# Forget heads: running sums spread through HBM instead of by transposes, and the logits projected before the first values

## The chip, the core and the metric

The program runs on one core of a Trainium2 chip. The core has a matrix engine (TensorE, PE in the profile, with a row of its own for the loading of weights, PEld), two engines for elementwise work (VectorE or DVE, ScalarE or ACT), GpSimd (POOL), and SyncE (SP), which here only issues transfers. Sixteen DMA engines move data between HBM and the on-chip memory. A transfer is issued from the queue of an engine: SP's for nearly all of them, ACT's for the results, POOL's for two. The metric is the device time of one execution in microseconds; the median of three runs is compared.

## What is computed

One block of a decoder for 256 positions and a model width of 2048, in float32. The part that the change touches is the forgetting attention: six heads of 128 columns, each with a logit per position that says how much is forgotten.

```python
h = rms_norm(x, g_mix[l])
proj = h @ w_in[l]
fq, fk, fv, f_logit, sq, sk, sv, mq, gates = jnp.split(proj, cuts, axis=-1)
...
log_f = jax.nn.log_sigmoid(f_logit.astype(jnp.float32) + b_forget[l].astype(jnp.float32))
...
c = jnp.cumsum(log_f, axis=-1)
...
    s = jnp.einsum('bhqd,bhkd->bhqk', q_blk, k).astype(jnp.float32) * scale
    s = s + c_blk[..., :, None] - c[..., None, :]
    s = jnp.where(key_pos[None, :] <= q_pos[:, None], s, -jnp.inf)
    p = jax.nn.softmax(s, axis=-1)
    return jnp.einsum('bhqk,bhkd->bhqd', p.astype(v.dtype), v)
```

So a head needs its running sum c twice: at the query's position, which is one number for each partition (queries lie on the partitions), and at the key's position, which is a row of 256 numbers that every partition must hold. Besides these six heads there are six stick-breaking heads, four heads over a memory of 256 tokens, three gates, an output projection, and a feed-forward part with a short convolution.

## The kernel before

**Products.** A float32 weight is used as the sum of two parts, `hi` and `lo`. `piece` (L136) loads 128 x 1024 numbers into `raw` through SP (L141), ACT rounds them to `hi` (L142), and DVE subtracts to get `lo` (L143). Each product of a tile is three matmuls (`three`, L328 to L330): high by high, low activation by high weight, high activation by `lo`. There are four buffers each of `raw`, `hi` and `lo`, so a load waits until DVE is through with the piece four places earlier. `product` runs the 2048 input columns in eight pieces of two tiles, which makes 24 such groups of matmuls for a result of 256 x 512.

**The order of the projections.** `proj` is called for the memory queries (`mq`), then for the forget heads' columns: f0, f1 and f2 are their queries and keys, f3 (512 columns) the values of heads 0 to 3, and f4 (262 columns) the values of heads 4 and 5 and the six logits. Then come s0, s1 and s2 (queries and keys of the stick-breaking heads), s3 and s4 (their values), and the gates g. In the profile the digits of such names are left out (`f`, `raw_f`, `s`).

**Work beside the products.** After each piece `product` calls `tick`. It moves on a background generator that loads pairs of tiles of later weights into `staged` (L301, SP), adds them up (L249 to L251, DVE) and stores the sums to HBM (L292, SP), and up to two (later three) of the waiting generators: transposes of finished queries and keys (`heads_T`), attention heads, and `running_sums`. A scheduler then lays out each engine's instructions from this order and the dependences; every engine and every DMA queue runs its own list strictly in order, and semaphores join the lists.

**A forget head before.** `running_sums` (L844) multiplies the log-sigmoids by triangles of ones on PE (L847 to L849), and DVE copies the result to `cq` (L850, L851), which holds the sums by query. `fox_head` then makes the row by key: DVE copies the head's column to 128 x 256 (L863), PE transposes its two halves against the identity into the bank `fa` (L868, two instructions), and ACT copies the result from there to `ck` (L871). PE's two score products (L869, L870) stand behind the transposes. DVE adds and subtracts the sums (L874), POOL masks the diagonal (L875), and the softmax, three transposes and the product with the values follow (`softmax_rows`, L882 to L885, `weighted`). The generators of the sums and of the heads are queued after f4, so they run beside s0 to s3.

**Another place that spreads a row.** The feed-forward part needs one scale per position in every partition. It writes 256 numbers of 4 bytes to HBM through POOL's queue (`rstd_row`, L1103) and loads them into all partitions from there (`rbc`, L1104). It is the one such pair in the program before.

Of the kernel before, what the change touches and what calls it, by code (L numbers as in the profile page):

```python
# [9 lines left out]
F32 = mybir.dt.float32  # L10
F32R = mybir.dt.float32r
AF = mybir.ActivationFunctionType
ALU = mybir.AluOpType
AX = mybir.AxisListType

P = 128
S = 256
NT = S // P
# [3 lines left out]
N_FOX, N_SB, N_MEM = 6, 6, 4  # L22
# [20 lines left out]
def hybrid_block(  # L43
# [25 lines left out]
    nc = tc.nc  # L69
# [12 lines left out]
    def bank(name):  # L82
        return pp.tile([P, 512], F32, tag="bank", name=name)
# [14 lines left out]
    def later(gen):  # L98
        waiting.append(gen)
# [18 lines left out]
    issued = set()  # L118

    def until(*names):  # L120
        while not issued.issuperset(names):
            yield
# [34 lines left out]
    def product(x_of, w, nk, n0, n, name):  # L157

        ps = [bank(f"{name}_{t}") for t in range(NT)]
        wv = w.rearrange("(k p) n -> p k n", p=P)  # L160
        for k in range(0, nk, 2):
            a = min(2, nk - k)
            wh, wl = piece(wv[:, k : k + a, n0 : n0 + n], a, n, f"{name}_{k}")
            order = [(j, t) for j in range(a) for t in range(NT)]
            if k + a == nk:
                order.sort(key=lambda jt: jt[1])
            for j, t in order:
                xk = x_of(k + j)
                xs_ = xk[:, t * P : (t + 1) * P], xk[:, S + t * P : S + (t + 1) * P]
                three(ps[t][:, :n], *xs_, (wh[:, j], wl[:, j]), k + j == 0, k + j == nk - 1)  # L170
            tick()
        return ps

    def split_to(dst, src):

        nc.scalar.copy(dst[..., :S], src)
        nc.vector.tensor_tensor(dst[..., S:], src, dst[..., :S].bitcast(F32), ALU.subtract)
# [57 lines left out]
    dram = ctx.enter_context(tc.tile_pool(name="dram", bufs=1, space=bass.MemoryType.DRAM))  # L235
# [250 lines left out]
    ident = cst.tile([P, P], F32, name="ident")  # L486
# [112 lines left out]
    rstd, rneg, rstd_m, rstd_f = (scales[:, i] for i in range(4))  # L599
# [7 lines left out]
    gp = mix.enter_context(tc.tile_pool(name="gp", bufs=3))  # L607

    def block(name, dt=F32):
        return bp.tile([P, 1024], dt, tag="blk", name=name)  # L610
# [4 lines left out]
    def rows_of(b):  # L615
        return b.rearrange("p (t n) -> p t n", t=NT)
# [26 lines left out]
    def heads_T(y, dst, gs, delay, name):  # L643

        yield delay
        for pr in range(2):
            ps = bank(f"hT_{name}_{pr}")
            for j in range(2):
                for t in range(NT):
                    h = 2 * pr + j  # L650
                    nc.tensor.transpose(
                        ps[:, j * S + t * P : j * S + (t + 1) * P], y[:, t, h * HD : (h + 1) * HD], ident
                    )
            out_v = dst[:, 2 * pr : 2 * pr + 2].rearrange("p h s -> p (h s)")
            if gs[pr] is None:
                nc.vector.tensor_copy(out_v, ps)
            else:
                nc.vector.tensor_scalar(out_v, ps, gs[pr], None, ALU.mult)
            if pr == 0:
                yield  # L660
        issued.add(name)
# [54 lines left out]
    for k in range(KT):  # L716
# [18 lines left out]
        for _ in range(0 if k < 3 else 1 if k < 8 else 3):  # L735
            if squares:
                j, t = squares.popleft()
# [16 lines left out]
    proj = lambda n0, n, name: product(xT, w_in[0], KT, n0, n, name)  # L754
    oT = op.tile([P, N_FOX + N_SB + N_MEM, 2 * S], F32R, tag="ot", name="oT")

    def softmax_rows(dst, src, name):
        nm = sm.tile([P, 1], F32, tag="nm", name=f"nm_{name}")
        nc.vector.tensor_reduce(nm, src, AX.X, ALU.max, negate=True)
        rs = sm.tile([P, 1], F32, tag="rs", name=f"rs_{name}")  # L760
        nc.scalar.activation(dst, src, AF.Exp, bias=nm, accum_out=rs)
        nc.vector.reciprocal(rs, rs)
        nc.vector.tensor_scalar(dst, dst, rs, None, ALU.mult)

    def weighted(pT, v, h, oh, o):

        c = slice((h % 4) * HD, (h % 4 + 1) * HD)
        vh = v[h // 4]
        nc.tensor.matmul(o[:, :S], lhsT=vh[:, 0, c], rhs=pT[:, :S], start=True, stop=False)
        nc.tensor.matmul(o[:, P:S], lhsT=vh[:, 1, c], rhs=pT[:, S : S + P], start=False, stop=True)  # L770
        split_to(oT[:, oh, :], o[:, :S])


    ps = proj(C_MQ, MEM_W, "mq")
# [40 lines left out]
    vf = [None] * 2  # L815
    for c in range(3):
        ps = proj(c * 512, 512, f"f{c}")
# [4 lines left out]
            for h in range(N_MEM):  # L822
                later(mem_head(h))
        later(heads_T(y, qk[c], gs, 2, f"f{c}"))
    ps = proj(1536, 512, "f3")
    vf[0] = rows_of(block("vf0"))
    for t in range(NT):
        nc.scalar.activation(vf[0][:, t], ps[t], AF.Copy, scale=rstd[:, t : t + 1])
    ps = proj(2048, 262, "f4")
    vf[1] = rows_of(block("vf1"))  # L830
    logits = cst.tile([P, 4, NT * N_FOX], F32, name="logits").rearrange("p i (t h) -> p i t h", t=NT)
    fl, lf, ab, cq = (logits[:, i] for i in range(4))
# [8 lines left out]
    nc.scalar.activation(ab, ab, AF.Ln, bias=1.0)  # L841
    nc.vector.scalar_tensor_tensor(lf, fl, 0.0, ab, ALU.min, ALU.subtract)

    def running_sums():  # L844
        yield 2
        cps = bank("cps")
        nc.tensor.matmul(cps[:, :N_FOX], lhsT=upto, rhs=lf[:, 0], start=True, stop=True)  # L847
        nc.tensor.matmul(cps[:, 8 : 8 + N_FOX], lhsT=ones, rhs=lf[:, 0], start=True, stop=False)
        nc.tensor.matmul(cps[:, 8 : 8 + N_FOX], lhsT=upto, rhs=lf[:, 1], start=False, stop=True)  # L849
        nc.vector.tensor_copy(cq[:, 0], cps[:, :N_FOX])  # L850
        nc.vector.tensor_copy(cq[:, 1], cps[:, 8 : 8 + N_FOX])  # L851
        issued.add("sums")

    def fox_head(h):
        yield from until("sums", "f0", "f1", "f2")
        q, k = qk[h // 4][:, h % 4], qk[(N_FOX + h) // 4][:, (N_FOX + h) % 4]
        b = block(f"fx_{h}")
        cb = b[:, :S].rearrange("p (j s) -> p j s", j=NT)
        ck = b[:, S : 2 * S]
        s = (b[:, 2 * S : 2 * S + P], b[:, 2 * S + P : 3 * S + P])  # L860
        pT = b[:, : 3 * P]

        nc.vector.tensor_copy(cb, cq[:, :, h : h + 1].to_broadcast([P, NT, P]))  # L863
        yield
        A = bank(f"fa_{h}")
        B = bank(f"fb_{h}")
        for j in range(NT):
            nc.tensor.transpose(A[:, j * P : (j + 1) * P], cb[:, j], ident)  # L868
        nc.tensor.matmul(B[:, :P], lhsT=q[:, :P], rhs=k[:, :P], start=True, stop=True)  # L869
        nc.tensor.matmul(A[:, S:], lhsT=q[:, P:], rhs=k, start=True, stop=True)  # L870
        nc.scalar.copy(ck, A[:, :S])  # L871
        for i, sp in enumerate((B[:, :P], A[:, S:])):
            nk = (i + 1) * P
            nc.vector.scalar_tensor_tensor(s[i], sp, cq[:, i, h : h + 1], ck[:, :nk], ALU.add, ALU.subtract)  # L874
            nc.gpsimd.affine_select(  # L875
                s[i][:, nk - P :], s[i][:, nk - P :], pattern=[[-1, P]], compare_op=ALU.is_ge,
                fill=NEG, base=0, channel_multiplier=1,
            )
            softmax_rows(s[i], s[i], f"f{h}_{i}")
        yield 3  # L880
        tp = B[:, P:]
        nc.tensor.transpose(tp[:, :P], s[0], ident)  # L882
        nc.tensor.transpose(tp[:, P : 2 * P], s[1][:, :P], ident)
        nc.tensor.transpose(tp[:, 2 * P :], s[1][:, P:], ident)
        nc.vector.tensor_copy(pT, tp)  # L885
        yield
        weighted(pT, vf, h, h, A)

    later(running_sums())
    for h in range(N_FOX):  # L890
        later(fox_head(h))

# [2 lines left out]
    for c in range(3):  # L895
        ps = proj(C_SB + c * 512, 512, f"s{c}")
# [52 lines left out]
    ps = proj(C_SB + 1536, 512, "s3")  # L949
# [4 lines left out]
    ps = proj(C_SB + 2048, 256, "s4")  # L954
# [56 lines left out]
    for m in range(2):  # L1011
        gate = []
        for b, plan in enumerate(g_plans[m]):
# [41 lines left out]
            if not plan:  # L1055
                biases()
                for n in range(2):
                    ps = proj(c0 + n * 512, 512, f"g{n}_{b}")
# [12 lines left out]
        for n in range(2):  # L1071
            acc = gate[branches[0][3]][n]
            for i, (w, k0, nk, b) in enumerate(branches):
                ps = product(lambda k: oT[:, k0 + k], w[0], nk, (2 * m + n) * 512, 512, f"b{2 * m + n}_{b}")
# [141 lines left out]
    for f0 in range(0, FT, 4):  # L1216
# [5 lines left out]
        for s in range(2):  # L1222
            ps = [bank(f"u{f0 + i}_{s}") for i in range(4)]
# [118 lines left out]
```

## Time and profile before

| what | value |
|---|---|
| three runs, us | 1461.80, 1462.06, 1462.67 (median 1462.06) |
| the profiled execution, us | 1461.49 |
| span from its first to its last instruction, us | 1459.8 |
| granted TensorE clock over the span | 1.000 |
| PE busy, share of the span | 1454.0 us, 100% |
| DVE, ACT, POOL busy | 1213.4 us, 850.0 us, 19.3 us |
| moved by DMA | 381.08 MB, 261 GB/s on average |

All times inside the program are microseconds from the span's start. A row of the view of groups or of one tile names line, engine, operation, result and operands, shape and count, with the duration of one. A row of the timeline gives start, duration, engine, line, operation and, in brackets, how long the engine stood idle before it and for what. In the view by stages each row is a stretch of time with the busy time of each engine in it, the granted clock, the share of the DMA engines' time that packets took, and the rate at which they moved data.

### The profile page before, as it was taken

What the parts mean: (1) busy time and instruction counts of PE and PEld (TensorE: products, weight loads), DVE (VectorE), ACT (ScalarE), POOL (GpSimd) and SP (SyncE); (2) the same over time, 40 slices, a digit from 0 to 9 for tenths busy, and PEclk for the clock granted to TensorE, in tenths of its full rate; (3) what the DMA queues carried; (4) which work ended last, traced back from release to release, by engine and by line L of the source; (5) the groups of instructions that cost most, each with busy time, mean ns of one, the idle gap of its engine ahead of it and who ended that gap; (6) DMA issues with size and microseconds to landing.
All of it is one profiled execution on the core that took longest, in us unless ns stands there. A gap on an engine that the chain in (4) does not pass through costs nothing.

```text
span 1459.8 us, 20547 instructions
## 1 busy us (share of the span) xinstructions
PE 1454.0 (100%) x7314; PEld 1230.1 (84%) x7314; DVE 1213.4 (83%) x1791; ACT 850.0 (58%) x1212; POOL 19.3 (1%) x48
## 2 busy tenths in 40 slices
PE   9999999999999999999999999999999999999998
PEld 7888888888888888888888888888888888888887
DVE  5778777776898899997887888888888877999878
ACT  6755454564564555545666556556556565676665
POOL 0000000010000000000000000000000000000000
PEclk9999999999999999999999999999999999999999
DMA  9697798777668576788877888888888866899995
GB/s 312 202 330 248 267 341 288 238 241 222 209 207 269 172 231 198 270 265 263 276 196 232 288 266 306 278 273 299 283 281 298 267 200 202 253 291 333 299 324 222
DMA packets 162534, 381.08 MB, mean 261 GB/s; under 512 B 12234, under 2 KB 27486, under 8 KB 158334
## 3 DMA queue, kind: packets, MB, share of 16 engines
q1 hardware_dynamic: 161022, 377.52, 78.9%
q10 hardware_dynamic: 1328, 2.11, 0.4%
q8 instruction: 57, 0.93, 0.3%
q14 instruction: 47, 0.39, 0.1%
q0 software_dynamic: 80, 0.13, 0.0%
HBM read 343.01 MB, written 36.70 MB: 260 GB/s over the span
## 4 chain that ended last, share of the span: by engine, by line
PE 97%; DVE 1%; DMA 1%; issue 0%; SPq 0%; ACT 0%; DVEq 0%; ACTq 0%
PE u L1231 22%; PE u L1232 11%; PE xd L329 3%; PE xd L330 3%; PE xd L328 3%; PE xg L330 3%; PE xg L329 3%; PE xg L328 3%; PE s L328 2%; PE s L330 2%; PE f L330 2%; PE f L328 2%; PE f L329 2%; PE s L329 2%; PE b L330 2%; PE b L328 2%
## 5 line engine op out<-in xcount | busy, mean ns | idle before, releaser
L1231 PE MATMUL u<-hT,hi_u 128*128 128x512 f32 x1232 | 428.3, 394 | 0.0
L1232 PE MATMUL u<-hT,lo_u 128*128 128x256 f32 x1232 | 341.3, 277 | 0.0
L1231 PEld LDWEIGHTS u<-hT,hi_u 128*128 128x128 f32 x1232 | 231.0, 188 | 53.8
L143 DVE TENSOR_TENSOR lo_u<-raw_u,hi_u 128x1024 fp32r<-128x1024 f32 x176 | 215.1, 1222 | 73.2 <-ACT hi_u L142 71.9
L142 ACT CAST hi_u<-raw_u 128x1024 fp32r<-128x1024 f32 x176 | 184.7, 1050 | 135.0 <-PE u L1231 106.7
L1232 PEld LDWEIGHTS u<-hT,lo_u 128*128 128x128 f32 x1232 | 231.2, 188 | 0.0
L323 DVE TENSOR_TENSOR lo_d<-raw_d,hi_d 128x1024 fp32r<-128x1024 f32 x88 | 106.7, 1222 | 16.2 <-ACT hi_d L322 13.8
L322 ACT CAST hi_d<-raw_d 128x1024 fp32r<-128x1024 f32 x88 | 91.7, 1053 | 38.8 <-PE xd L329 17.8
L322 ACT CAST hi_g<-raw_g 128x1024 fp32r<-128x1024 f32 (+1 forms) x80 | 77.1, 972 | 48.9 <-PE xg L329 19.2
L323 DVE TENSOR_TENSOR lo_g<-raw_g,hi_g 128x1024 fp32r<-128x1024 f32 (+1 forms) x80 | 88.6, 1119 | 4.1 <-ACT hi_g L322 4.1
L142 ACT CAST hi_f<-raw_f 128x1024 fp32r<-128x1024 f32 (+1 forms) x40 | 38.5, 967 | 51.8 <-PE f L329 42.8
L330 PE MATMUL xg<-lo_g,xT 128*128 128x512 f32 x175 | 68.1, 389 | 0.0
L329 PE MATMUL xg<-hi_g,xT 128*128 128x512 f32 x175 | 68.1, 389 | 0.0
L328 PE MATMUL xg<-hi_g,xT 128*128 128x512 f32 x175 | 68.1, 389 | 0.0
L143 DVE TENSOR_TENSOR lo_f<-raw_f,hi_f 128x1024 fp32r<-128x1024 f32 (+1 forms) x40 | 44.6, 1118 | 22.3 <-ACT hi_f L142 21.7
L143 DVE TENSOR_TENSOR lo_s<-raw_s,hi_s 128x1024 fp32r<-128x1024 f32 (+1 forms) x40 | 44.7, 1117 | 20.9 <-ACT hi_s L142 20.9
L1231 PE MATMUL u<-hT_rest,hi_u 128*128 128x512 f32 x176 | 62.0, 394 | 0.0
L142 ACT CAST hi_b<-raw_b 128x1024 fp32r<-128x1024 f32 x32 | 33.6, 1051 | 45.2 <-DMA raw_b<-in_w_br_fox_dram 15.8
L142 ACT CAST hi_s<-raw_s 128x1024 fp32r<-128x1024 f32 (+1 forms) x40 | 38.4, 961 | 36.8 <-PE s L329 23.9
L1182 ACT ACTIVATE y<-u,taps 128x256 f32<-128x256 f32 x88 | 49.6, 596 | 16.3 <-DVE u L1177 16.2
L330 PE MATMUL xd<-lo_d,aT 128*128 128x512 f32 x148 | 57.6, 389 | 0.0
L328 PE MATMUL xd<-hi_d,aT 128*128 128x512 f32 x148 | 57.6, 389 | 0.0
(520 smaller groups left out, 3473.1 us busy)
## 6 DMA issues: line engine op xcount, KB each, us to landing
raw_u<-in_w_up_dram SPq DMA_DIRECT2D x176, 512.0 KB, 4.5
raw_g<-in_w_in_dram SPq DMA_DIRECT2D x96, 512.0 KB, 4.4
raw_d<-in_w_down_dram SPq DMA_DIRECT2D x63, 512.0 KB, 5.4
pre_d<-in_w_down_dram SPq DMA_DIRECT2D x17, 1024.0 KB, 6.2
kept_d<-pre_d SPq DMA_DIRECT2D x17, 1024.0 KB, 6.2
raw_f<-in_w_in_dram SPq DMA_DIRECT2D x32, 512.0 KB, 4.9
raw_s<-in_w_in_dram SPq DMA_DIRECT2D x32, 512.0 KB, 5.2
raw_t_d<-kept_d SPq DMA_DIRECT2D x25, 512.0 KB, 5.8
```

The lines of the kernel that those rows point to most:

```text
L142: pin(nc.scalar.copy(hi[:, :m], raw[:, :m]))
L143: pin(nc.vector.tensor_tensor(lo[:, :m], raw[:, :m], hi[:, :m].bitcast(F32), ALU.subtract))
L322: nc.scalar.copy(hi[:, :n], src)
L323: nc.vector.tensor_tensor(lo[:, :n], src, hi[:, :n].bitcast(F32), ALU.subtract)
L328: fix(nc.tensor.matmul(o, lhsT=ah, rhs=w[0], start=first, stop=False))
L329: fix(nc.tensor.matmul(o, lhsT=al, rhs=w[0], start=False, stop=False))
L330: fix(nc.tensor.matmul(o, lhsT=ah, rhs=w[1], start=False, stop=last))
L1182: nc.scalar.activation(y, u[:, 2:], AF.Identity, scale=tap(2), bias=tap(3))
L1231: nc.tensor.matmul(ps[i], lhsT=hi[:, j, c], rhs=hT(k + j), start=first, stop=False)
L1232: nc.tensor.matmul(ps[i][:, :S], lhsT=lo[:, j, c], rhs=hT(k + j)[:, :S], start=False, stop=last)
```

## The change

Three things are done.

1. The projection f4 and the logits that come from it are placed ahead of f3. `running_sums` is queued right behind f4, and so runs beside f3; the six heads are queued after f3.
2. At the end of `running_sums` the sums go to HBM and back, in two parts: heads 0 to 3 (`ck_row4`, 4 KB) and heads 4 and 5 (`ck_row2`, 2 KB). The first two transfers write 256 runs of 16 bytes and 256 runs of 8 bytes. The other two load the whole row into each of the 128 partitions: `ck4`, 512 KB, into the one buffer tagged `pre`, and `ck2`, 256 KB, into one of the three tagged `bg`. All four are issued from POOL's queue, and each load waits for its own write.
3. A head no longer makes its row: DVE's spreading copy, the two transposes, ACT's copy and one step of waiting are gone, and the subtraction reads the loaded row. Before the product with the values a head checks that f3 has been written out.

```diff
-    ps = proj(1536, 512, "f3")
-    vf[0] = rows_of(block("vf0"))
-    for t in range(NT):
-        nc.scalar.activation(vf[0][:, t], ps[t], AF.Copy, scale=rstd[:, t : t + 1])
     ps = proj(2048, 262, "f4")
...
+    ck = [None] * N_FOX
+
     def running_sums():
         yield 2
...
         nc.vector.tensor_copy(cq[:, 1], cps[:, 8 : 8 + N_FOX])
+        for h0, n, tag, bufs in ((0, 4, "pre", 1), (4, 2, "bg", 3)):
+            row = dram.tile([S, n], F32, tag=f"ck_row{n}", name=f"ck_row{n}")
+            nc.gpsimd.dma_start(row.rearrange("(t p) h -> p t h", t=NT), cq[:, :, h0 : h0 + n])
+            every = gp.tile([P, S * n], F32, tag=tag, bufs=bufs, name=f"ck{n}")
+            nc.gpsimd.dma_start(every, row.rearrange("s h -> (s h)").partition_broadcast(P))
+            for h in range(n):
+                ck[h0 + h] = every.rearrange("p (s h) -> p h s", h=n)[:, h]
+        yield 5
         issued.add("sums")
+
+    later(running_sums())
+    ps = proj(1536, 512, "f3")
+    vf[0] = rows_of(block("vf0"))
+    for t in range(NT):
+        nc.scalar.activation(vf[0][:, t], ps[t], AF.Copy, scale=rstd[:, t : t + 1])
+    issued.add("vf0")
 
     def fox_head(h):
         yield from until("sums", "f0", "f1", "f2")
         q, k = qk[h // 4][:, h % 4], qk[(N_FOX + h) // 4][:, (N_FOX + h) % 4]
         b = block(f"fx_{h}")
-        cb = b[:, :S].rearrange("p (j s) -> p j s", j=NT)
-        ck = b[:, S : 2 * S]
...
-        nc.vector.tensor_copy(cb, cq[:, :, h : h + 1].to_broadcast([P, NT, P]))
-        yield
         A = bank(f"fa_{h}")
         B = bank(f"fb_{h}")
-        for j in range(NT):
-            nc.tensor.transpose(A[:, j * P : (j + 1) * P], cb[:, j], ident)
         nc.tensor.matmul(B[:, :P], lhsT=q[:, :P], rhs=k[:, :P], start=True, stop=True)
         nc.tensor.matmul(A[:, S:], lhsT=q[:, P:], rhs=k, start=True, stop=True)
-        nc.scalar.copy(ck, A[:, :S])
...
-            nc.vector.scalar_tensor_tensor(s[i], sp, cq[:, i, h : h + 1], ck[:, :nk], ALU.add, ALU.subtract)
+            nc.vector.scalar_tensor_tensor(s[i], sp, cq[:, i, h : h + 1], ck[h][:, :nk], ALU.add, ALU.subtract)
...
         nc.vector.tensor_copy(pT, tp)
         yield
+        yield from until("vf0")
         weighted(pT, vf, h, h, A)
 
-    later(running_sums())
     for h in range(N_FOX):
         later(fox_head(h))
```

The lists of the engines move as follows. In these rows the digits of a name are whole (`lo_f4_8` is the lo part of f4's piece that starts at tile 8), and the last number is that of the buffer.

First DVE, in the list of before, from the last `lo` that is made early for the projection behind f2 to the next one:

```order
L143 TENSOR_TENSOR lo_f3_6_1616<-raw_f3_6_1614,hi_f3_6_1615 128x1024
L631 TENSOR_REDUCE hss_f2_1524<-sq_f2_0_1525 128x4
L631 TENSOR_REDUCE hss_f2_1524<-sq_f2_1_1528 128x4
L658 TENSOR_SCALAR qk_fox0_1051<-hT_f0_1_1565,gh_109 128x512
L573 TENSOR_SCALAR nwa_f2_1532<-hss_f2_1524 128x8
L658 TENSOR_SCALAR qk_fox1_1313<-hT_f1_1_1571,gh_109 128x512
L576 TENSOR_TENSOR nwt_f2_1533<-nwy_f2_1534 128x8
L249 TENSOR_TENSOR staged_861<-staged_861 128x1024
L577 SCALAR_TENSOR_TENSOR nwt_f2_1533<-nwt_f2_1533,nwa_f2_1532 128x8
L143 TENSOR_TENSOR lo_f3_8_1637<-raw_f3_8_1635,hi_f3_8_1636 128x1024
```

The same place of DVE's list after the change, where the projection behind f2 is f4:

```order
L658 TENSOR_SCALAR qk_fox0_1051<-hT_f0_0_1508,gh_109 128x512
L658 TENSOR_SCALAR qk_fox1_1313<-hT_f1_0_1514,gh_109 128x512
L249 TENSOR_TENSOR staged_861<-staged_861 128x1024
L631 TENSOR_REDUCE hss_f2_1524<-sq_f2_0_1525 128x4
L631 TENSOR_REDUCE hss_f2_1524<-sq_f2_1_1528 128x4
L658 TENSOR_SCALAR qk_fox0_1051<-hT_f0_1_1565,gh_109 128x512
L573 TENSOR_SCALAR nwa_f2_1532<-hss_f2_1524 128x8
L658 TENSOR_SCALAR qk_fox1_1313<-hT_f1_1_1571,gh_109 128x512
L576 TENSOR_TENSOR nwt_f2_1533<-nwy_f2_1534 128x8
L250 TENSOR_TENSOR staged_861<-staged_861 128x512
L577 SCALAR_TENSOR_TENSOR nwt_f2_1533<-nwt_f2_1533,nwa_f2_1532 128x8
L143 TENSOR_TENSOR lo_f4_8_1637<-raw_f4_8_1635,hi_f4_8_1636 128x524
```

The evictions of heads (L658), the norms of f2 and the background sums stand now between pieces of f4, whose matmuls are half as wide as those of f3.

Second PE, in the list of before, where head 0's scores stand behind the piece s0_8:

```order
L330 MATMUL s0_1_1891<-lo_s0_8_1977,xT_432 128x512
L868 MATMUL fa_0_1993<-ident_78,fx_0_1973 128x128 x2
L869 MATMUL fb_0_1994<-qk_fox1_1313,qk_fox0_1051 128x128
L870 MATMUL fa_0_1993<-qk_fox1_1313,qk_fox0_1051 128x256
L328 MATMUL s0_0_1890<-hi_s0_10_2023,xT_432 128x512
```

The same scores in PE's list after the change:

```order
L330 MATMUL s0_1_1905<-lo_s0_2_1926,xT_432 128x512
L876 MATMUL fb_0_1944<-qk_fox1_1313,qk_fox0_1051 128x128
L877 MATMUL fa_0_1943<-qk_fox1_1313,qk_fox0_1051 128x256
L328 MATMUL s0_0_1904<-hi_s0_4_1968,xT_432 128x512
L329 MATMUL s0_0_1904<-hi_s0_4_1968,xT_432 128x512
```

The two transposes are gone, and the scores stand three pieces earlier, behind s0_2.

Third DVE again after the change, where the sums are copied out of PSUM and where they are used (`ck4` is the loaded row of heads 0 to 3):

```order
L848 COPY logits_1723<-cps_1809 128x6
L849 COPY logits_1723<-cps_1809 128x6
L143 TENSOR_TENSOR lo_f3_8_1825<-raw_f3_8_1823,hi_f3_8_1824 128x1024
L143 TENSOR_TENSOR lo_f3_10_1845<-raw_f3_10_1843,hi_f3_10_1844 128x1024
L143 TENSOR_TENSOR lo_f3_12_1864<-raw_f3_12_1862,hi_f3_12_1863 128x1024
L143 TENSOR_TENSOR lo_f3_14_1882<-raw_f3_14_1880,hi_f3_14_1881 128x1024
```

```order
L143 TENSOR_TENSOR lo_s0_4_1969<-raw_s0_4_1967,hi_s0_4_1968 128x1024
L143 TENSOR_TENSOR lo_s0_6_2014<-raw_s0_6_2012,hi_s0_6_2013 128x1024
L880 SCALAR_TENSOR_TENSOR fx_0_1942<-fb_0_1944,logits_1723,ck4_1817 128x128
L880 SCALAR_TENSOR_TENSOR fx_0_1942<-fa_0_1943,logits_1723,ck4_1817 128x256
L759 TENSOR_REDUCE nm_f0_0_1951<-fx_0_1942 128x1
L759 TENSOR_REDUCE nm_f0_1_1961<-fx_0_1942 128x1
```

The copies have moved from the middle of s0 to the middle of f3, and the four transfers wait for them; the first use of a loaded row stands on DVE between lo_s0_6 and lo_s0_8. On POOL's list the four transfers stand ahead of the mask of head 0. On SP's list the loads of the gates' biases (`bg`, L1019 before, L1025 after), which stood among the loads of the memory's weights at the start, stand now among those of s1 and s2, and the second and third of them directly ahead of the load of s2_12.

## The prediction

> **What bounds the kernel now.** I read the busy times first, then the chain that ended last, then the stretch from f3 to the middle of s1 by stages.
>
> ```profile
> span 1459.8 us, 20547 instructions
> PE 1454.0 (100%) x7314; PEld 1230.1 (84%) x7314; DVE 1213.4 (83%) x1791; ACT 850.0 (58%) x1212; POOL 19.3 (1%) x48
> PE 97%; DVE 1%; DMA 1%; issue 0%; SPq 0%; ACT 0%; DVEq 0%; ACTq 0%
> ```
>
> PE is busy for all but 6 us, and 97% of the chain is its own list. So two things count: matmul time taken off PE, and any wait that makes PE stand. Work taken from DVE or ACT is worth nothing by itself. The stages, with their DMA share and rate in the last two columns:
>
> ```profile
> 156.00:168.00 12.00, 12.00 (x63) 10.09 (x61) 11.28 (x19) 6.83 (x10) 0.00 (x0) 1.00 0.63 221
> 168.00:180.50 12.50, 12.50 (x61) 10.33 (x60) 10.14 (x15) 3.64 (x5) 0.00 (x0) 1.00 0.78 261
> 180.50:192.30 11.80, 11.80 (x98) 11.76 (x97) 7.76 (x10) 6.18 (x9) 0.00 (x0) 1.00 0.92 316
> 192.30:203.80 11.50, 11.50 (x56) 9.59 (x54) 5.80 (x8) 5.50 (x10) 0.00 (x0) 1.00 0.98 366
> 203.80:216.00 12.20, 12.20 (x60) 10.14 (x60) 11.56 (x29) 7.18 (x15) 2.35 (x4) 1.00 1.01 373
> ```
>
> The first two are f3, the third f4, the rest s0 and the start of s1. Because f4 uses its pieces twice as fast, the loads fall behind, and for the 24 us behind it the DMA engines are full at 366 to 373 GB/s. How near PE comes to standing there:
>
> ```profile
> ACT hi_s L142 <- DMA raw_s<-in_w_in_dram: 7.5, 8, 2.7
> 189.81 1.22 DVE L143 TENSOR_TENSOR lo_s<-raw_s,hi_s 128x1024 fp32r<-128x1024 f32 x1
> 192.78 0.39 PE L330 MATMUL s<-lo_s,xT 128*128 128x512 f32 x1
> ```
>
> ACT waits eight times for these loads. The first `lo` of s0 ends at 191.03 and is used at 192.78, a lead of 1.75 us. That is the least cover that I find there, and PE does not stand.
>
> **The change part by part: the transposes.** One head in the timeline of PE, and the two copies that go with it:
>
> ```profile
> 206.46 0.39 PE L330 MATMUL s<-lo_s,xT 128*128 128x512 f32 x1
> 206.69 0.38 PE L868 MATMUL fa<-ident,fx 128*128 128x128 f32 x2
> 206.90 0.39 PE L869 MATMUL fb<-qk_fox,qk_fox 128*128 128x128 f32 x2
> L863 DVE COPY fx<-logits x6: 274/286/289, 205.3 to 243.8; 128x256 f32<-128x256 f32 x6
> L871 ACT COPY fx<-fa x6: 351/373/374, 207.8 to 257.6; 128x256 f32<-128x256 f32 x6
> ```
>
> From L868 to L869 is 0.21 us of PE's list; six heads give **-1.26 us**, all on the path. DVE loses 6 x 0.29 and ACT 6 x 0.37 us; both lie beside PE and count nothing. The heads also start three pieces earlier and take a step less each; PE runs the same instructions, so I count that at nothing too. The check for f3's values costs nothing, since they are written out before a head reaches it.
>
> **The exchange of f3 and f4.** PE's matmuls are the same; what changes is what DVE must do beside them.
>
> ```profile
> 156.88 0.47 PE L328 MATMUL f<-hi_f,xT 128*128 128x512 f32 x1
> 157.39 0.74 DVE L658 TENSOR_SCALAR qk_fox<-hT_f,gh 128x512 f32<-128x512 f32 x1
> 163.05 1.22 DVE L143 TENSOR_TENSOR lo_f<-raw_f,hi_f 128x1024 fp32r<-128x1024 f32 x1
> 164.87 1.28 DVE L638 TENSOR_TENSOR y_f<-y_f,hr_f 128x512 f32<-128x512 f32 x2
> L143 DVE TENSOR_TENSOR lo_f<-raw_f,hi_f x13: 694/705/1219, 158.0 to 187.3; 128x524 fp32r<-128x524 f32 x8, 128x1024 fp32r<-128x1024 f32 x5
> ```
>
> Behind f2, DVE has evictions, norms and background sums; the fifth `lo` of f3 starts at 163.05. After the change that place loses a long `lo` (about 1.1 us to the next start) and gains a background sum (about 0.6), so f4's fifth `lo` ends near 162.5 + 0.7 = 163.2. A piece of f4 takes 11.8 / 8 = 1.47 us on PE, and four of them, with the eight transposes between, bring PE to its fifth `lo` at about 163.3: just in time. The next `lo` has a sum and two products of the norm ahead of it and comes about 2.6 us later, against 1.5 us of matmuls and some transposes that PE puts between. I take **+0.5 us**, and 0 to 1.5 as bounds.
>
> **The row through HBM.** The trace has one such pair, `rstd_row` and `rbc`:
>
> ```profile
> 761.13 0.86 POOL L1103 DMA_DIRECT2D rstd_row<-scales  x1 [421.83 <-DVE scales L578]
> 769.55 0.57 POOL L1104 DMA_DIRECT2D rbc<-rstd_row  x1 [7.55 <-DMA rstd_row<-scales]
> rbc<-rstd_row POOLq DMA_DIRECT2D x1, 128.0 KB, 7.2
> rstd_row<-scales POOLq DMA_DIRECT2D x1, 1.0 KB, 8.1
> 753.00:763.00 10.00, 10.00 (x60) 8.73 (x59) 6.76 (x16) 9.18 (x16) 0.86 (x1) 1.00 0.74 235
> 763.00:772.00 9.00, 9.00 (x54) 7.86 (x53) 4.91 (x7) 3.34 (x6) 0.57 (x1) 1.00 0.69 61
> 772.00:780.00 8.00, 8.00 (x48) 7.00 (x47) 3.87 (x4) 3.11 (x3) 0.00 (x0) 1.00 0.85 297
> ```
>
> The write of 1 KB takes 8.1 us, and while it runs everything else slows: 61 GB/s where the stretches around it have 235 and 297. It isn't that there was nothing to move. The loads of the feed-forward weights that SP issued from 740 to 762 us, then those from 762 to 770 us, and what ACT saw of them:
>
> ```profile
> DMA to landing us min/median/max: 3.6/3.6/4.0
> DMA to landing us min/median/max: 11.2/11.4/11.6
> ACT hi_u L142 <- DMA raw_u<-in_w_up_dram: 6.7, 2, 5.7
> ```
>
> Each load lands 7.8 us later than the ones before. Or by the rate: 9 us x (1 - 61 / 366) = **7.5 us** of a full DMA lost to one write of 256 small runs. There PE didn't stand, because its `hi` and `lo` were several pieces of some 3 us ahead. In f3, behind f4, they are not.
>
> The new writes are two, of 256 runs each, issued 0.86 us apart. PE starts f3 near 156 + 0.9 + 11.8 = 169 us; the copies of the sums stand on DVE behind the fourth `lo` of f3, near 178, so the writes run from about 180. That is 11 us behind f4's end, where the same distance in the program before is the row 203.80:216.00 with a full DMA. Lost DMA time is bounded by 0 (the larger runs pass at once) and 15 us (two writes in turn, each at the measured price). I take one price, 7.5, because the two overlap and because count and route are those of the measured one. The loads into all partitions add 0.79 MB, at 366 GB/s 2.1 us, less a cover of 1.75: PE stands for 7.5 + 2.1 - 1.75 = **+7.85 us** (bounds 0.35 and 15.35). Nothing gives this back, as the DMA is full before and after it.
>
> The Trainium skill, "DMA: Bandwidth & Descriptors", section "Anatomy of one DMA — SWDGE (gpsimd) path", fits a transfer from POOL's queue as 2.0 us plus its bytes at 436 GB/s. By that the write of 1 KB would take 2.0 us; the trace has 8.1, so here the trace decides. With the page's price and no slowing of others the sum would be that of the first rival. The same page's "Specifications" says that pieces under 512 B are read, modified and written; that speaks for a price by the number of runs, since 4, 8 and 16 bytes are alike below it.
>
> **What waits, and what is queued behind it.** POOL's four issues (2 x 0.86 + 2 x 0.57 us) and the wait for the writes stand ahead of head 0's mask:
>
> ```profile
> 208.59 0.69 POOL L875 TENSOR_SCALAR_AFFINE_SELECT fx<-fx 128x128 f32<-128x128 f32 x2 [206.44 <-DVE fx L874]
> ```
>
> POOL has been idle for 206 us there, which covers them. The row of heads 0 to 3 lands at about 178 + 8.1 + 0.6 + 7.2 + 1.8 = 196 us (the larger load takes 0.66 MB / 366 GB/s more). Its first use stands behind `lo_s0_6` and head 0's scores, PE's time 169 + 22 + 5.5 = 196.5 at the earliest. Should the row be late, DVE stands, and every `lo` from s0_8 on behind it; but the same slow DMA delays PE, so I add nothing. On SP's list two bias loads now stand ahead of s2_12's load and wait for head 5's subtraction; loads run several pieces ahead in that stretch, so nothing, at most 1 us.
>
> **The sum.** 1461.49 - 1.26 + 0.5 + 7.85 = 1468.6 for the profiled execution, whose span is 1459.8; it lies 0.57 under the median of the runs, so 1469.2, given as **1469**.
>
> **The rivals.** *The writes slow nothing, or are hidden* (the other side: not slower). The run of 16 or 8 bytes may pass quickly, or PE's lead may be larger than 1.75 us at that moment. Then -1.26 + 0.5 + 0.35 gives 1461.7. For it: one event is all that shows the slowing. Against: rate, landing and ACT's wait all agree on it. It decides below about 3 us of lost DMA. Chance 0.22.
> *Half the price* (runs four times as long, spread over 4 KB instead of 1): 3.75 lost, +3.3 in all, 1465.4. Chance 0.15.
> *One price*, my forecast: 1469. Chance 0.42.
> *Two in turn*: 15 us lost, 1476.7. For it: one queue carries both, and 512 runs are twice 256. Chance 0.18.
> *Faster by over 0.2%*, 2.9 us, about what a measurement of this kernel can tell from no change: the transposes give 1.26, and I know no other matmul time that goes. Chance 0.03.
>
> **Range and chances.** From the no-loss case to the doubled one, 1461 to 1477; about 0.15 lie outside. A third of the half-price case is within 0.2%, so: faster 0.03, same 0.26, slower 0.71. The likeliest case's own range is 1466 to 1472.
>
> **What would show it.** Right: a stretch of 6 to 15 us behind the writes with the rate well under 366 GB/s, ACT's waits for `raw_f` or `raw_s` longer by several us, and PE idle at `hi` or `lo` of late f3 or early s0; then heads of two products without L868. Wrong: the rate stays up there (the first rival), or PE stands at the products with the values or at head 0 because the row came late, or PE stands in f4 for several us behind DVE.

## The result, and the profile after

| what | before | after |
|---|---|---|
| median of 21 runs each, us | 1461.58 (1461.01 to 1465.18) | 1464.15 (1462.80 to 1466.80) |
| ratio, 95% interval | | 1.0018 [1.0012, 1.0024] |
| the profiled execution, us | 1461.49 | 1463.10 |
| its span, us | 1459.8 | 1461.4 |

The changed kernel is slower by 2.6 us, clear of the noise and on the side that I forecast, but by little more than a third of the 7 us that I forecast (1469 against the 1462.06 known then): 1464.15, inside the range of 1461 to 1477. The profiled execution is one of the faster ones of after (1.6 us over that of before), so what it shows lost is somewhat under the usual.

The page of after, its span, busy times and the chain of waits:

```profile
span 1461.4 us, 20527 instructions
PE 1454.0 (99%) x7302; PEld 1229.0 (84%) x7302; DVE 1211.1 (83%) x1785; ACT 848.7 (58%) x1206; POOL 20.8 (1%) x52
PE 95%; issue 2%; DVE 1%; DMA 1%; SPq 0%; POOL 0%; ACT 0%; POOLq 0%; DVEq 0%; ACTq 0%
```

PE has its twelve transposes fewer (7302 for 7314) and is still the bound. All its waits between 150 and 300 us (engine and line, what it waited for, us, times, longest); before, there were none:

```profile
PE f L328 <- ACT hi_f L142: 0.9, 1, 0.9
PE f L330 <- DVE lo_f L143: 0.5, 1, 0.5
PE s L330 <- DVE lo_s L143: 0.3, 1, 0.3
```

The first two stand at the last piece of f3, where PE's timeline reads:

```profile
190.52 0.39 PE L330 MATMUL f<-lo_f,xT 128*128 128x512 f32 x1
191.80 0.50 PE L328 MATMUL f<-hi_f,xT_rest 128*128 128x512 f32 x1 [0.89 <-ACT hi_f L142]
192.14 0.40 PE L329 MATMUL f<-hi_f,xT_rest 128*128 128x512 f32 x1
193.06 0.50 PE L330 MATMUL f<-lo_f,xT_rest 128*128 128x512 f32 x1 [0.52 <-DVE lo_f L143]
193.40 0.40 PE L328 MATMUL f<-hi_f,xT_rest 128*128 128x512 f32 x1
193.63 0.39 PE L329 MATMUL f<-hi_f,xT_rest 128*128 128x512 f32 x1
```

By the starts, 190.52 to 191.80 is 1.28 us where a step is 0.23, and 192.14 to 193.06 is 0.92: 1.05 + 0.69 us lost. That is more than the waits say, because a wait is counted from the end of the matmul before, which is 0.39 us behind that one's start, while the next matmul usually starts 0.23 us behind that start. The matmul behind a wait also takes 0.34 instead of 0.23 to its successor, another 0.11 each time. At 207.92 to 208.63, in s0, another 0.48 go. At the feed-forward part PE is 1.8 us later than before (745.0 and 743.2 us); with the transposes' 1.26 that is some 3 us lost in this profile.

What was going on then: POOL's transfers in its timeline, how long they took to land (the list of transfers; kind, count, size, us), and the stretches around them, DMA share and GB/s in the last two columns:

```profile
179.89 1.59 POOL L852 DMA_DIRECT2D ck_row<-logits  x2 [177.75 <-DVE logits L849]
187.09 0.57 POOL L854 DMA_DIRECT2D ck<-ck_row  x1 [5.61 <-DMA ck_row<-logits]
190.85 0.55 POOL L854 DMA_DIRECT2D ck<-ck_row  x1 [3.19 <-DMA ck_row<-logits]
```

```profile
ck<-ck_row POOLq DMA_DIRECT2D x1, 512.0 KB, 7.5
ck<-ck_row POOLq DMA_DIRECT2D x1, 256.0 KB, 6.6
ck_row<-logits POOLq DMA_DIRECT2D x1, 4.0 KB, 6.9
ck_row<-logits POOLq DMA_DIRECT2D x1, 2.0 KB, 9.8
```

```profile
168.00:180.00 12.00, 12.00 (x68) 10.28 (x67) 11.17 (x20) 6.74 (x10) 0.11 (x1) 1.00 0.98 376
182.00:194.00 12.00, 10.59 (x46) 8.15 (x45) 4.67 (x4) 4.36 (x5) 1.12 (x2) 1.00 0.99 279
```

The share of the DMA engines' time stays at 0.98 and 0.99 while the rate falls from 376 to 279 GB/s. Against 366 that is 12 x (1 - 279 / 366) = 2.9 us of DMA time; against the 328 to 347 of the kernels below that have no crowded writes in this stretch, mean 336, it is 2.0 us.

### The profile page after: what moved, and what is told of

The parts are those of the page before. It is cut to its first block, busy times and chain, and to the rows that moved or that the text cites. A ratio compares the mean times of both kernels' runs of the same rounds, so it can differ in the third digit from the quotient of the medians.

```text
span 1461.4 us, 20527 instructions
## 1 busy us (share of the span) xinstructions
PE 1454.0 (99%) x7302; PEld 1229.0 (84%) x7302; DVE 1211.1 (83%) x1785; ACT 848.7 (58%) x1206; POOL 20.8 (1%) x52
## 4 chain that ended last, share of the span: by engine, by line
PE 95%; issue 2%; DVE 1%; DMA 1%; SPq 0%; POOL 0%; ACT 0%; POOLq 0%; DVEq 0%; ACTq 0%
PE u L1237 22%; PE u L1238 11%; PE xg L330 4%; PE xg L328 4%; PE xg L329 4%; PE xd L330 3%; PE xd L328 3%; PE xd L329 3%; PE b L330 2%; PE b L328 2%; PE b L329 2%; PE s L328 2%; PE s L330 2%; PE s L329 2%; PE yd L330 2%
## 5 line engine op out<-in xcount | busy, mean ns | idle before, releaser
L142 ACT CAST hi_b<-raw_b 128x1024 fp32r<-128x1024 f32 x32 | 33.7, 1053 | 44.9 <-PE b L329 15.7
```

The costliest lines, as they stand in the source:

```text
L142: pin(nc.scalar.copy(hi[:, :m], raw[:, :m]))
```

## Experiments

Each median stands beside that of the kernel before, measured together with it. First, which part of the change costs. Theory W names the two writes, X the exchange of f3 and f4, L the loads into all partitions.

**The exchange alone.** The trip is taken out and the heads make their rows as before:

```diff
-        for h0, n, tag, bufs in ((0, 4, "pre", 1), (4, 2, "bg", 3)):
...
     def fox_head(h):
+        nc.vector.tensor_copy(cb, cq[:, :, h : h + 1].to_broadcast([P, NT, P]))
+        yield
...
+        for j in range(NT):
+            nc.tensor.transpose(A[:, j * P : (j + 1) * P], cb[:, j], ident)
...
+        nc.scalar.copy(ck, A[:, :S])
```

> The exchange of f3 and f4 alone: the sums run beside f3, but each head makes its row with DVE's copy, two transposes and ACT's copy as before, and no row goes through HBM. Theory W (the two writes of small runs take DMA time from the loads, and PE stands for it): no loss is left, 1461.6 to 1462.1 against 1461.6 before. Theory X (the exchange itself starves PE: loads and the lo parts come late behind f4): the loss stays and the transposes come back, 1464.2 + 1.26 = 1465.4. Theory L (the 0.79 MB of loads into all partitions are the cost): 1461.6 to 1462.1, as under W.

Measured: 1461.93 against 1461.89, ratio 0.9999 [0.9991, 1.0008]. Theory X falls. PE has no wait between 100 and 300 us. ACT waits for the loads of f3 there too, and it costs nothing:

```profile
ACT hi_f L142 <- DMA raw_f<-in_w_in_dram: 12.0, 7, 3.8
```

In after the same row has 15.7 us. So a long wait of ACT's for loads, by itself, doesn't tell that PE stands.

**The trip alone**, the two writes and two loads in the order of before:

```diff
         nc.vector.tensor_copy(cq[:, 1], cps[:, 8 : 8 + N_FOX])
+        for h0, n, tag, bufs in ((0, 4, "pre", 1), (4, 2, "bg", 3)):
...
+        yield 5
         issued.add("sums")
```

> The trip through HBM alone, in the order of before (f3, then f4; the sums beside s0, the four transfers from about 204 us on, heads a few pieces later). Theory W: the DMA engines are full there too (1.01 of their time at 204 to 216 us before), so the writes cost as in the changed kernel, some 3 us of DMA time less the lead, and the transposes give 1.26 back: 1462.5 to 1464. Theory X: nothing is exchanged, so the transposes' gain is left, 1460.3. Theory L: 2.1 us of load time less a lead of 1.75 and less 1.26: 1460.5 to 1461.

Measured: 1464.28 against 1461.89, ratio 1.0016 [1.0007, 1.0026], just above the 1464 that theory W allowed. The whole loss of the change comes with the trip, in another place of the program. PE stands once, at a `lo` of s0 some 20 us behind the writes:

```profile
231.99 0.50 PE L330 MATMUL s<-lo_s,xT 128*128 128x512 f32 x1 [1.98 <-DVE lo_s L143]
```

**The change without the writes:**

```diff
-            nc.gpsimd.dma_start(row.rearrange("(t p) h -> p t h", t=NT), cq[:, :, h0 : h0 + n])
-            nc.gpsimd.dma_start(every, row.rearrange("s h -> (s h)").partition_broadcast(P))
+            nc.gpsimd.tensor_copy(every[:, :1], cq[:, 0, :1])
+            nc.gpsimd.dma_start(every, b_gate[0, 0, : S * n].partition_broadcast(P))
```

> The changed kernel without the two writes; the loads into all partitions read rows of the gates' bias instead, behind a one-column copy on POOL that waits for the sums. The heads' forgetting term by key is therefore not computed from the logits. Theory W: the loss goes with the writes, and with only the loads left (2.1 us, lead 1.75) PE stands under 1 us: 1460.5 to 1461.5. Theory X: nothing changes, 1464.2. Theory L: nothing changes, 1464.2, and the loads start some 7 us earlier.

Measured: 1461.08 against 1461.89, ratio 0.9993 [0.9985, 1.0002]. The loads alone cost nothing that can be seen; theory L falls. The writes are what costs.

**The same trip with long runs.** One transpose of the sums on PE makes 12 rows of 128, and the writes carry 8 and 4 runs of 512 bytes:

```diff
+        nc.tensor.transpose(cps[: NT * N_FOX, P : 2 * P], cflat, ident)
+        cT = block("cT")[: NT * N_FOX, :P]
+        nc.vector.tensor_copy(cT, cps[: NT * N_FOX, P : 2 * P])
...
-            row = dram.tile([S, n], F32, tag=f"ck_row{n}", name=f"ck_row{n}")
-            nc.gpsimd.dma_start(row.rearrange("(t p) h -> p t h", t=NT), cq[:, :, h0 : h0 + n])
+            row = dram.tile([n * NT, P], F32, tag=f"ck_row{n}", name=f"ck_row{n}")
+            nc.gpsimd.dma_start(row, cT[h0 * NT : (h0 + n) * NT])
```

> The changed kernel with the same trip, but the sums are transposed once on PE first (12 columns, one instruction) and copied by DVE to 12 partitions, so that the two writes carry 8 and 4 runs of 512 bytes instead of 256 runs of 16 and 256 of 8. Theory W: the slowing goes with the number of small runs, so it goes away: 1460.7 to 1461.7. If instead any write from POOL's queue slows the others, whatever its runs, 1463.5 to 1464.5. Theories X and L: 1464.2 + 0.1.

> The kernel of the long runs once more, unchanged, to narrow its interval against the kernel before: 1460.8, 0.9992 of before, if the eleven transposes' 1.15 us are what it gains; 1461.5 to 1462 if the first comparison was luck.

Measured: 1460.81 against 1461.89, ratio 0.9992 [0.9983, 1.0001], and the second time 1461.71 against 1461.67, ratio 0.9999 [0.9990, 1.0009]. The loss is gone. Whether the eleven transposes' 1.15 us are gained isn't shown: the intervals hold both that and nothing. The stretch 182 to 194 us of this kernel, to be set beside that of after:

```profile
182.00:194.00 12.00, 12.00 (x55) 9.84 (x54) 8.56 (x10) 6.37 (x8) 2.31 (x4) 1.00 0.99 335
```

The same DMA share carries 335 GB/s, and PE is busy for all 12 us (in after, 10.59).

**The long runs in the order of before**, the same edit made to the trip alone:

```diff
-            nc.gpsimd.dma_start(row.rearrange("(t p) h -> p t h", t=NT), cq[:, :, h0 : h0 + n])
+            nc.gpsimd.dma_start(row, cT[h0 * NT : (h0 + n) * NT])
```

> The trip through HBM in the order of before (as in the trip alone), with the sums transposed once and written in 8 and 4 runs of 512 bytes. If crowded runs were all that the trip alone lost by, its 2.4 us go away and the twelve transposes less one are left: 1460.5 to 1461.2, as with the exchange. If the waits of DVE for late scores or rows cost there, 1462 to 1464.

Measured: 1461.13 against 1461.67, ratio 0.9999 [0.9990, 1.0008]. The trip alone loses nothing any more either.

**ACT's queue for the writes:**

```diff
-            nc.gpsimd.dma_start(row.rearrange("(t p) h -> p t h", t=NT), cq[:, :, h0 : h0 + n])
+            nc.scalar.dma_start(row.rearrange("(t p) h -> p t h", t=NT), cq[:, :, h0 : h0 + n])
```

> The changed kernel with the two writes issued from ACT's queue instead of POOL's; the loads stay on POOL's. If the slowing belongs to POOL's queue, it goes away: 1460.5 to 1461.5. If it belongs to the small runs, it stays: 1463.5 to 1465.

Measured: 1466.46 against 1462.18, ratio 1.0027 [1.0017, 1.0037]. The cost doesn't belong to POOL's queue. It is above the 1465 that I expected at most; whether it is larger than from POOL's isn't shown, since the interval overlaps that of after.

**Each write done twice**, the second time to a row that nobody reads:

```diff
             nc.gpsimd.dma_start(row.rearrange("(t p) h -> p t h", t=NT), cq[:, :, h0 : h0 + n])
+            again = dram.tile([S, n], F32, tag=f"again{n}", name=f"again{n}")
+            nc.gpsimd.dma_start(again.rearrange("(t p) h -> p t h", t=NT), cq[:, :, h0 : h0 + n])
```

> The changed kernel with each of the two writes done a second time to a row that nobody reads. If the lost DMA time adds up (2.9 us for the first pair by the rate) and PE pays for all of it, now that its lead is used up, 1464.2 + 2.9 = 1467.1, between 1466 and 1468. If the writes overlap and only the first pair matters, 1464.2 to 1465.

Measured: 1467.20 against 1462.18, ratio 1.0029 [1.0018, 1.0040]. The second pair costs about 0.0011 x 1462 = 1.6 us more by the ratios and 3.0 by the medians. That is what adding prices would give, or nearly, but it isn't shown: the intervals of the two ratios overlap.

Now why two writes cost less than my price for one. **My price at this place:** the kernel of the long runs with a write of 256 runs of 4 bytes into 1 KB, like `rstd_row`, ahead of its own:

```diff
+            if h0 == 0:
+                extra = dram.tile([NT, P], F32, tag="extra", name="extra")
+                nc.gpsimd.dma_start(extra.rearrange("t p -> p t"), cq[:, :, 0])
```

> The kernel of the long runs (1460.8, PE stands 0.1 us) with one more write ahead of its two: 256 runs of 4 bytes packed into 1 KB, as the write measured before, which nobody reads. If my price of 7.5 us of DMA time for such a write holds at this place, PE stands for 5.75 to 7.5 us: 1466.5 to 1468.3. If a write costs here what one of the changed kernel's did, about half of the 2.9 us that their two took, 1461 to 1462.3.

Measured: 1466.93 against 1462.18, ratio 1.0030 [1.0020, 1.0040]; over the kernel of the long runs 1466.93 - 1461.25 (the median of its 22 runs) = 5.7 us. So in time a write of this kind costs here about what I had priced. The stretch behind it, in an execution of 1469.91 us:

```profile
188.00:190.00 2.00, 2.00 (x11) 1.65 (x10) 0.91 (x1) 1.05 (x1) 0.00 (x0) 1.00 2.09 164
190.00:192.00 2.00, 2.00 (x11) 1.65 (x10) 0.32 (x1) 0.00 (x0) 0.00 (x0) 1.00 0.78 93
192.00:194.00 2.00, 1.06 (x5) 0.56 (x3) 0.00 (x0) 0.00 (x0) 0.00 (x0) 1.00 0.77 89
194.00:196.00 2.00, 0.11 (x1) 0.11 (x1) 0.13 (x1) 1.04 (x1) 0.68 (x2) 0.83 0.78 113
```

In these 8 us the mean rate is 115 GB/s: 8 x (1 - 115 / 366) = 5.5 us of DMA time lost, and PE is nearly empty at the end of them. But not all that PE loses is waiting. The third column from the end is the granted clock, which falls to 0.83 in the last row; behind it PE goes on at half the clock:

```profile
195.89 0.80 PE L328 MATMUL f<-hi_f,xT_rest 128*128 128x512 f32 x1 [2.83 <-ACT hi_f L142]
199.02 0.63 PE L328 MATMUL f<-hi_f,xT_rest 128*128 128x512 f32 x1
199.45 0.63 PE L329 MATMUL f<-hi_f,xT_rest 128*128 128x512 f32 x1
198.00:200.00 2.00, 2.00 (x6) 1.51 (x6) 1.34 (x2) 1.72 (x2) 0.00 (x0) 0.50 1.04 409
200.00:202.00 2.00, 2.00 (x6) 1.52 (x5) 2.00 (x4) 1.26 (x3) 0.00 (x0) 0.50 1.03 420
```

A step takes 0.43 us there instead of 0.23, with the DMA back at 409 to 420 GB/s. From 195.89 to 202.30 PE makes 14 steps in 6.41 us, where 14 x 0.23 = 3.2: about as much is lost to the clock as to the wait before it. So the agreement with my price is partly luck. The traces of two more kernels show the same: the trip alone behind its wait of 2.0 us (0.50 from 234 to 236 us), and the writes from ACT's queue behind a wait of 3.0 (0.50 from 194 to 196). In the changed kernel, with 0.9 us for the longest wait, and in the kernel that writes twice, with 1.4, the clock stays at 1.00. Whether other executions of the changed kernel lose by the clock isn't shown, as only this trace of it was kept.

The changed kernel's writes differ from this one by the size of their runs and by what they are spread over, so the next two kernels vary that.

**Single writes, one by one**, beside the feed-forward part of the kernel before. `probe` copies a finished tile on POOL and writes one list of runs from the copy to HBM:

```diff
             ys[f] = y
+            if f in probes:
+                probe(f, y)
```

> The kernel before with twelve extra writes to HBM that nobody reads, one in each 34 us of the feed-forward part, where the loads come one by one with spare DMA time; each source is a copy on POOL of a finished tile. In order: 256 runs of 4 bytes packed into 1 KB (as the one measured write); 256 of 16 bytes packed into 4 KB; 256 of 4 bytes, each at the start of its own 512 bytes; 128 of 512 bytes; 12 of 512 bytes; 256 of 4 bytes packed, from ACT's queue; 256 of 4 packed again; 256 of 8 packed; 256 of 16 and at once 256 of 8; 128 of 4 packed; 256 of 16 from ACT's queue; 256 of 4 packed once more. Theory N (the price goes by the number of small runs): every write of 256 takes some 8 us to land and delays the loads beside it by 6 to 8 us, 128 runs half of that, the pair 15 us. Theory P (the price goes by how many runs share the same few hundred bytes of HBM): 8 us for 4 bytes packed, half or less for 16 packed, and 2 to 3 us for the spaced ones. Theory Q (POOL's queue is what slows): the two from ACT's queue land in 2 to 3 us and delay nothing. 12 runs of 512 bytes: 2 to 3 us under all.

> Again extra writes beside the feed-forward part of the kernel before, one in each 45 us. In order, all of 256 runs from POOL's queue but where it says otherwise: 4 bytes at steps of 64; 4 bytes at steps of 32; 4 bytes at steps of 128; 16 bytes at steps of 64; 8 bytes packed; 16 packed and at once 8 packed; 128 runs of 4 bytes packed (512 bytes in all); 64 bytes packed; 16 bytes packed from ACT's queue. So far: 10.4 us to land for 4 bytes packed, 6.2 for 16 packed, 4.4 for 4 bytes at steps of 512. If the crowding within one stretch of HBM sets the price, the order is 4 packed, 8 packed (7 to 9 us), 16 packed, and everything at steps of 64 or more takes 4 to 5 us and delays no load. If runs that fall on the same 512 bytes wait for one another and different ones go side by side, 128 runs of 4 packed take as long as 256 (10 us); if the count of crowded runs matters, half of the excess (7 us).

The part has 44 column tiles, so only the first six of the first list took place. The list of transfers of the first kernel, in the order of the writes, each taken from a stretch of its own:

```profile
prow<-probe POOLq DMA_DIRECT2D x1, 1.0 KB, 10.4
prow<-probe POOLq DMA_DIRECT2D x1, 4.0 KB, 6.2
prow<-probe POOLq DMA_DIRECT2D x1, 1.0 KB, 4.4
prow<-probe POOLq DMA_DIRECT2D x1, 64.0 KB, 4.4
prow<-probe POOLq DMA_DIRECT2D x1, 6.0 KB, 3.9
prow<-probe ACTq DMA_DIRECT2D x1, 1.0 KB, 9.2
```

And of the second, leaving out the fourth (16 bytes at steps of 64: 4.3):

```profile
prow<-probe POOLq DMA_DIRECT2D x1, 1.0 KB, 5.2
prow<-probe POOLq DMA_DIRECT2D x1, 1.0 KB, 4.6
prow<-probe POOLq DMA_DIRECT2D x1, 1.0 KB, 5.6
...
prow<-probe POOLq DMA_DIRECT2D x1, 2.0 KB, 7.8
prow<-probe POOLq DMA_DIRECT2D x1, 4.0 KB, 4.9
qrow<-probe POOLq DMA_DIRECT2D x1, 2.0 KB, 7.1
prow<-probe POOLq DMA_DIRECT2D x1, 0.5 KB, 11.4
prow<-probe POOLq DMA_DIRECT2D x1, 16.0 KB, 4.6
prow<-probe ACTq DMA_DIRECT2D x1, 4.0 KB, 2.6
```

| runs, and how they lie in HBM | us to land | the loads of 512 KB beside it, median us |
|---|---|---|
| 256 of 4 bytes, packed | 10.4 (POOL), 9.2 (ACT) | 9.0 (POOL), 9.7 (ACT) |
| 128 of 4 bytes, packed into 512 | 11.4 | |
| 256 of 8 bytes, packed | 7.8 | |
| 256 of 16 and at once 256 of 8, packed | 4.9 and 7.1 | 6.4 |
| 256 of 16 bytes, packed | 6.2 (POOL), 2.6 (ACT) | 4.1 (POOL), 4.8 (ACT) |
| 256 of 4 bytes at steps of 32, 64, 128, 512 | 4.6, 5.2, 5.6, 4.4 | 4.8, 4.4, 4.2, 4.8 |
| 256 of 16 bytes at steps of 64 | 4.3 | 4.1 |
| 256 of 64 bytes, packed | 4.6 | 4.4 |
| 128, 12 of 512 bytes | 4.4, 3.9 | 4.3, 4.8 |

Each row is one event; where the last field is empty, no landing beside the write was read off. The number of runs doesn't set the price: 256 runs of 4 bytes take 10.4 us packed and 4.4 to 5.6 spread out, and 128 packed take as long as 256. Nor does the queue, for 4 bytes. What it goes with is how many runs crowd into the same few bytes of HBM: 4 bytes packed cost most, 8 packed less, 16 packed little or nothing, and from a step of 32 on it takes 4.4 to 5.6 us, with the loads beside it at 4.2 to 4.8. How long the stretch is within which runs get in each other's way isn't settled by these: 64 and 512 bytes both fit.

**Crowding at the full place.** To the kernel of the long runs come the changed kernel's two writes, unread, once packed (as below) and once with rows of 16 numbers in place of n, so that each run stands at the start of its own 64 bytes:

```diff
+        nc.vector.tensor_copy(fl[:, 0], cps[:, :N_FOX])
+        nc.vector.tensor_copy(fl[:, 1], cps[:, 8 : 8 + N_FOX])
...
+            extra = dram.tile([S, n], F32, tag=f"extra{n}", name=f"extra{n}")
+            nc.gpsimd.dma_start(extra.rearrange("(t p) h -> p t h", t=NT)[:, :, :n], fl[:, :, h0 : h0 + n])
```

> The kernel of the long runs with the changed kernel's two writes added, to rows that nobody reads (256 runs of 16 bytes packed into 4 KB, 256 of 8 packed into 2 KB; DVE makes two tiny copies more). Whether the price goes by the number of runs or by their crowding, the changed kernel's loss comes back: 1463.3 to 1465.5.

> The same two added writes, the same 256 runs of 16 and of 8 bytes, but each run at the start of its own 64 bytes (16 KB each). If crowding sets the price at this full place of the DMA too, nothing is lost: 1461 to 1462.2, within 0.5 us of the kernel of the long runs. If the number of runs does, it is as with the packed ones, 1463.3 to 1465.5.

Measured: packed 1465.29 against 1462.05, ratio 1.0022 [1.0013, 1.0031]; spaced 1461.29, ratio 1.0000 [0.9991, 1.0009]. Two kernels with the same count and sizes of runs at the same place, 4.0 us apart by the medians. The stretches of the packed one:

```profile
190.00:192.00 2.00, 2.00 (x11) 1.65 (x10) 2.00 (x2) 0.03 (x1) 0.00 (x0) 1.00 1.75 134
192.00:194.00 2.00, 2.00 (x10) 1.69 (x9) 0.95 (x1) 1.02 (x1) 0.58 (x1) 1.00 0.60 39
194.00:196.00 2.00, 2.00 (x10) 1.65 (x9) 1.59 (x3) 1.64 (x2) 0.55 (x1) 1.00 0.40 31
```

And of the spaced one:

```profile
190.00:192.00 2.00, 2.00 (x10) 1.68 (x9) 2.00 (x3) 1.05 (x1) 0.44 (x1) 1.00 0.90 307
192.00:194.00 2.00, 2.00 (x10) 1.65 (x10) 2.00 (x3) 1.53 (x3) 0.00 (x0) 1.00 1.02 419
194.00:196.00 2.00, 2.00 (x11) 1.65 (x10) 1.41 (x2) 0.68 (x2) 0.00 (x0) 1.00 1.06 335
```

Between 192 and 196 us the packed writes leave 31 to 39 GB/s, the spaced ones 335 to 419. So crowding is the cause here too. Which of the two writes costs, that of 16 or that of 8 bytes, was not tried singly; the table speaks for that of 8.

## Why the prediction was wrong in size

**The step that failed** is the price of the writes: "I take one price, 7.5, because the two overlap and because count and route are those of the measured one". Count and route were alike, and neither sets the price. The measured write had runs of 4 bytes packed into 1 KB; the new ones have 16 and 8. At the same place of the program the one costs 5.7 us over the kernel of the long runs, the two new ones together 1465.29 - 1461.25 = 4.0, though the intervals of the two ratios, 1.0030 and 1.0022, overlap. The DMA time lost in the changed kernel is 2.0 to 2.9 us, not 7.5, and PE lost some 3 us in its trace (2.6 + 1.26 = 3.8 by the medians) where I had 7.85.

The rival *half the price* had this reason in its bracket ("runs four times as long, spread over 4 KB instead of 1"), 3.75 us lost and 1465.4; measured 1464.15 it is the nearest of the cases. That it came near is luck in the figure: the reason points the way the single writes did, but nothing made it a half. I gave it 0.15 against 0.42 because only one event was there to go by, and I leaned on the count. The page "DMA: Bandwidth & Descriptors" of the Trainium skill, section "Specifications", has pieces under 512 bytes read, modified and written, and I used it for a price by the number of runs; here 256 pieces of 4 bytes landed in 10.4 us or in 4.4, by their spacing, so the count of such pieces, which was my reading and not the page's, doesn't give the price.

**What was right.** That such writes slow the other transfers, that the DMA is full behind f4, and that PE therefore stands at `hi` and `lo` of the last piece of f3: the waits are there, at 191.80 and 193.06. The writes start at 179.89 us, as worked out (180). The row of heads 0 to 3 lands at 187.09 + 7.5 = 194.6 (forecast 196), and its first use isn't late. In the sum, 2.9 us lost + 2.1 for the loads - 1.75 of lead gives 3.25; PE lost some 3 us in the profiled execution. The loads alone cost nothing that could be seen, as 2.1 - 1.75 = 0.35 has it. In their trace the first `lo` of s0 ends at 193.83 and is used at 194.31, a lead of 0.48 us; with the exchange alone these are 191.63 and 193.95, a lead of 2.32. The loads take 1.8 us of the lead there, near the 2.1 of the sum. The writes without the loads were not tried.

**The smaller terms.** The transposes' -1.26 us is off PE's list, but no kernel shows it as time gained beyond its interval. The +0.5 us for DVE in f4 came out at nothing that can be seen, with the exchange alone at 0.9999; but it was as near as worked out, since f4's fifth `lo` ends at 164.03 and is used at 164.09. Waits that I had named as dangers, the row arriving late and the bias loads on SP, left no wait of PE's in the profile.

**What takes the gain.** The change does what it says on PE; it loses by a transfer of 6 KB that no busy time shows, since it runs where the DMA is full and PE's lead over the loads is small.

## What to carry to other kernels

Before spreading a few numbers through HBM, look at how the runs of the write lie there, and not at its bytes: many runs of 4 or 8 bytes side by side held up the other transfers for several microseconds here, while a transpose that makes them long, or a step of 32 bytes or more (64 where the DMA is full), took that away. Such a write costs time where the DMA is full and the bound engine has little lead; there take the rate in GB/s as the gauge, not the busy share, and look at the granted clock behind a wait of PE before putting all of a loss down to the wait. And when a price rests on one event, ask which of its properties the new case shares before multiplying.

## What the runs showed of the hardware that I had not expected

- 128 runs of 4 bytes packed into 512 bytes took 11.4 us to land, as long as 256 into 1 KB (8.1 to 10.4), and 256 at steps of 32 took 4.6.
- While crowded writes ran, the rate fell to 31 to 164 GB/s in stretches of 2 us whose DMA share read anything from 0.40 to 2.09, and to 279 over 12 us of the changed kernel at a share of 0.99; a busy share doesn't tell moving from being held up.
- The 16-byte packed write took 6.2 us alone from POOL's queue, 4.9 in a pair, and 2.6 from ACT's, one event each; why they differ is open, as is why ACT's queue didn't help at the full place.
- Behind single waits of PE of 2.0, 2.8 and 3.0 us the granted clock fell to 0.50 for about 3 to 6 us; behind waits of up to 1.4 us it stayed at 1.00.
- After a wait of PE the next matmul came 0.34 us later instead of 0.23 (191.80 to 192.14, and 193.06 to 193.40).
